# Last output tile in units of 512, 384 and 128 columns, epsilon as the logarithm's bias, a shorter Newton step, and a last pass of 640 and 384

## The chip, the core and the metric

One core of one Trainium2 chip runs the whole program in one launch. The metric is the device time of an execution in microseconds (us). The kernel before took 283.74 us (median of three runs, 282.71 to 284.28).

## What is computed

One step of a hybrid decoder trunk of depth 1. A prompt of 512 tokens and eight running sequences of one token each go through an input projection, a gated linear attention and a dilated sliding-window attention, and both mixers' outputs (`mix`, 1024 columns, 512 from each) go through one output projection and a layer norm. The change touches that last part alone:

```
mix = jnp.concatenate([o_a * silu(ga), o_b * silu(gb)], axis=-1)
y = jnp.einsum('bte,ed->btd', mix.astype(x.dtype), w_out)
x_new = layer_norm(DEEPNORM_ALPHA * x + y, ln_g, ln_b)

def layer_norm(x, g, b):
    mu = jnp.mean(xf, axis=-1, keepdims=True)
    var = jnp.mean(jnp.square(xf - mu), axis=-1, keepdims=True)
    return ((xf - mu) * lax.rsqrt(var + LN_EPS) * g + b)
```

All values are 32-bit floats, LN_EPS is 1e-5, and the norm's row of g and b is 1024 long.

## The kernel before

**Order of work.** The program is written as many small generators ("tasks"), each of which yields instructions and waits for marks that others set. A planner in the file (`Plan.run`, line 305) holds a cost for each instruction and, at every step, issues the ready instruction with the earliest start that it works out; ties go by each task's priority. So each engine's order is fixed when the program is built, by the planner's costs, and every instruction is recorded at one line (366). All matmuls of the large projections come from one task, `dense` (line 691), in a written order; the other engines' work falls between as the planner finds it ready.

**Matmuls.** Weights and activations are split into a high and a low part, and each product is three matmuls (`three`, line 618): high by high, high by low, low by high. With eight blocks of 128 in the contraction, a result tile is 24 matmuls into one PSUM bank.

**The output projection.** The 512 prompt tokens are four tiles of 128, t = 0 to 3. Tiles 0 and 1 are computed transposed (`out_first`, names ps_yf, feat_y, ps_yt). Tiles 2 and 3 come last of all matmuls, by `out_unit(t, c, w)` (line 1494): 128 tokens by w columns from column c, the activations (mha, mla, mhb, mlb) as the stationary operand and the weights (hi_wo, lo_wo) as the moving one, 24 matmuls of w columns each. Line 749 gives the units: tile 2 in two of 512, tile 3 in 512, 256 and 256.

**After a unit.** `out_evac` (line 1546), on VectorE: y = ALPHA * y + PSUM in one instruction for the unit, then one bn_stats for each 256 columns (GW) into `stats`, four of six numbers each for a row. The fourth adds `norm(t)` (line 1593): bn_aggr gives mean and variance (`mv`), and `rsqrt` (line 395) makes 1/sqrt(var + eps) in `rstd`. In the branch that the norm uses (`between` is given) VectorE adds eps to the variance, and ScalarE does Ln, Exp(-0.5 x), then a Newton step of four: Square, times x, times -0.5 plus 1.5, times the estimate. `between` is `centre`, which on VectorE does (y - mean) * gamma meanwhile. Last, VectorE does y * rstd + beta and the store is issued on SP's queue. For t = 3 the centring and the last pass are in two halves of 512 columns, each half with its own store; for the other tiles each is one instruction of 1024.

`rsqrt` without `between` (all on VectorE after Exp) serves the head norms and the eight sample rows (line 1587); that branch computes the same before and after.

Of the kernel before, what the change touches and what calls it, by code (L numbers as in the profile page):

```python
# [16 lines left out]
AF = mybir.ActivationFunctionType  # L17
ALU = mybir.AluOpType
AX = mybir.AxisListType

P = 128
# [119 lines left out]
def size(x):  # L141

    return math.prod(c for _, c in x.ap[1:])
# [51 lines left out]
class Plan:  # L195
# [14 lines left out]
    def add(self, gen, prio):  # L210
        self.seq += 1
        self.tasks.append(Task(gen, prio, self.seq))
# [158 lines left out]
def trunk(ctx: ExitStack, tc: tile.TileContext, xT, xp, xs, state, ck, cv, w_in, wab, gnorm,  # L371
# [17 lines left out]
    def bank(tag, name):  # L389
        return Need(tag, name, [P, 512])  # L390

    def cst(name, shape, dt=F32):
        return const.tile(shape, dt, name=name)

    def rsqrt(o, x, scale, eps, between=None):

        t = yield Need("m", "newton", [P, size(x)])
        t = t[:x.ap[0][1]]
        yield V.tensor_scalar(x, x, scale, eps, op0=ALU.mult, op1=ALU.add)
        yield S.activation(o, x, AF.Ln)  # L400
        yield S.activation(o, o, AF.Exp, scale=-0.5)
        if between:

            add(between, 5)
            yield S.activation(t, o, AF.Square)
            yield S.mul(t, t, x)
            yield S.activation(t, t, AF.Copy, scale=-0.5, bias=1.5)
            yield S.mul(o, o, t)
        else:
            yield V.tensor_tensor(t, o, o, op=ALU.mult)  # L410
            yield V.tensor_tensor(t, t, x, op=ALU.mult)
            yield V.tensor_scalar(x, o, -0.5, None, op0=ALU.mult)
            yield V.scalar_tensor_tensor(o, t, -3.0, x, op0=ALU.add, op1=ALU.mult)
        free(t)
# [113 lines left out]
    zw = plan.alloc(Need("t1", "zw", [P, KT, 32]))  # L528
    wz = plan.alloc(Need("t1", "wz", [P, 256]))
    one16 = cst("one16", [P, 1])  # L530

    def clear():

# [68 lines left out]

    def fills():
        yield V.memset(rb.bitcast(F32)[64:66], 1.0)
        yield At("const")
        raw = B["rb_raw"]
        yield S.copy(rb[:64], raw)
        yield V.tensor_tensor(rb[32:64], raw[32:], rb[32:64].bitcast(F32), op=ALU.subtract)
        free(raw)
        mark("rb")  # L610

        for key, shape in (("ks0", [P, 2, NP]), ("ks1", [P, 2, NP]), ("near", [P, 2, 8, 64])):
            B[key] = yield Need("g", key, shape)
            yield G.memset(B[key], 0.0)
            mark("zero_" + key)
# [75 lines left out]
    def dense():  # L691
        for _ in range(N_WARM):
            yield T.matmul(warm_ps, warm[:, :P], warm, start=True, stop=True)
        free(warm_ps)
        free(warm)

        pk = {}
        for i in range(2):
            for u in range(2):
                pk[i, u] = yield bank("ds"[i], f"ps_ka{i}{u}")  # L700
        for k in range(KT):
            for u in range(2):
                yield At("kas", k + 1)
                yield At("xs", k + 1 + (u if k == 0 else 1))
                for i in range(2):
                    yield from three(pk[i, u][:, :TW[u]], k, halves(k, u, groups[f"ka{i}"]))
        for x in ka_hl:
            free(*x)

        pz = yield bank(("t", "s"), "ps_za")  # L710
        yield At("zw")
        yield Batch(T.matmul(pz[j * 32:j * 32 + 32, :QN[j]], zw[:, k, :], xraw[k // 2][:, k % 2, Q0[j]:Q0[j] + QN[j]],
                             start=k == 0, stop=k == KT - 1, skip_group_check=True)
                    for k in range(KT) for j in range(TT))
        free(zw, *xraw)
        add(gate_decay(pz), 10)
        yield from make("ka", Need("g", "ka", [P, 2, NP]), 3)
        yield from make("qa", Need("g", "qa", [P, 2, NP]), 2)
        for i in range(2):
            for u in range(2):  # L720
                add(into("ka", ka_s, i, 1.0)(pk[i, u], u), 2)
        for i in range(2):
            yield from feature(groups[f"qa{i}"], into("qa", qa_s, i, 0.125))
        for x in ("qh0", "ql0", "qh1", "ql1"):
            yield from make(x, Need("g", x, [P, 4, 256], F32R), 4)
        for i in range(4):
            yield from feature(groups[f"qb{i}"], parts("q", q_s, i, 0.125))
        for i in range(4):
            yield from make(f"kp{i}", Need("g", f"kp{i}", [P, 2, 512], F32R), 2)
            yield from feature(groups[f"kb{i}"], parts("k", k_s, i, 1.0))  # L730
        for u in range(2):
            yield from make(f"v{u}", Need("g", f"v{u}", [P, 2, 512]))
        for i in range(2):
            yield from token(groups[f"vb{i}"], *vb_into(i))
        yield from gates("gb", gb_s)
        for u in range(2):
            yield from make(f"va{u}", Need("g", f"va{u}", [P, 2, 512]))
        for i in range(2):
            yield from token(groups[f"va{i}"], *va_into(i))
        yield from gates("ga", ga_s)  # L740
        free(*xt)
        for t in range(TT):
            add(residual(t), 8)
        add(residual_sample(), 8)
        units = [(g, f) for g in range(4) for f in range(2)]
        yield from out_first(*units[:5])
        for x in units[5:]:
            yield from out_first(x)
        for t, c, w in ((2, 0, 512), (2, 512, 512), (3, 0, 512), (3, 512, GW), (3, 768, GW)):
            yield from out_unit(t, c, w)  # L750


# [723 lines left out]
    def ln_rows():  # L1476
        yield At("y0_done", 1)
        for n, src in (("gamma", ln_g), ("beta", ln_b)):
            B[n] = yield Need("g", n, [P, DM])
            yield D.dma_start(B[n], src.to_broadcast([P, DM]))  # L1480
            mark("ln")

    def residual(t):
        if t in (2, 3):
            yield At("y0_done", 4)
        else:
            yield At("wo0_", 1)
        y = yield Need("g", f"y{t}", [P, DM])
        B["y", t] = y
        B["stats", t] = cst(f"stats{t}", [P, 4, 6])  # L1490
        yield D.dma_start(y, xp[t * P:t * P + P, :])
        mark(f"y{t}")

    def out_unit(t, c, w):
        u, tl, cs = t // 2, slice((t % 2) * P, (t % 2) * P + P), slice(c % 512, c % 512 + w)
        g = wo[c // 512]
        ps = yield bank("d", f"ps_y{t}{c // GW}")
        for k in range(KT):
            yield g.at(k)
            yield At(f"mix_b{u}{k}") if k < 4 else At(f"mix_a{u}", t % 2 + 1)  # L1500
            mh, ml = (B[f"m{x}{'ba'[k // 4]}{u}"][:, k % 4, tl] for x in "hl")
            hi, lo = g.hi[k][:, cs], g.lo[k][:, cs]
            yield from three(ps[:, :w], k, ((mh, hi), (mh, lo), (ml, hi)))
        add(out_evac(t, c // GW, ps[:, :w]), 2)

    def out_first(*units):

# [19 lines left out]
    def out_turn(g, f, ps):  # L1527
        feat = yield Need("t1", "feat_y", [P, GW])
        yield copy(feat, ps[:, :GW])
        yield copy(yts[:, 2 * g + f, :], ps[:, GW:TW[0]])  # L1530
        mark("yts")
        free(ps)
        if f == 0:
            yield from make(f"yt{g}", bank("t", f"ps_yt{g}"))
        else:
            yield At(f"yt{g}")
        for t in range(2):
            yield T.transpose(B[f"yt{g}"][:, t * GW + f * P:t * GW + f * P + P], feat[:, t * P:t * P + P], ident)
        free(feat)
        mark(f"yt_in{g}")  # L1540
        if plan.marks[f"yt_in{g}"] == 2:
            plan.share(B[f"yt{g}"], 2)
            for t in range(2):
                add(out_evac(t, g, B[f"yt{g}"][:, t * GW:t * GW + GW]), 2)

    def out_evac(t, g, ps):
        yield At(f"y{t}")
        y, st = B["y", t], B["stats", t]
        c = slice(g * GW, g * GW + size(ps))
        yield V.scalar_tensor_tensor(y[:, c], y[:, c], ALPHA, ps, op0=ALU.mult, op1=ALU.add)  # L1550
        free(ps)
        for i in range(g, g + size(ps) // GW):
            yield V.bn_stats(st[:, i, :], y[:, i * GW:i * GW + GW])
            mark(f"y{t}_done")
        if plan.marks[f"y{t}_done"] == 4:
            add(norm(t), 7 if t == 3 else 9)

    def residual_sample():
# [34 lines left out]
    def norm(t):  # L1593
        y, st = B["y", t], B["stats", t]
        mv, rstd = cst(f"mv{t}", [P, 2]), cst(f"rstd{t}", [P, 1])
        yield V.bn_aggr(mv, st.rearrange("p a b -> p (a b)"))
        ws = (512, 512) if t == 3 else (DM,)
        cs = [slice(sum(ws[:i]), sum(ws[:i]) + w) for i, w in enumerate(ws)]

        def centre():  # L1600
# [7 lines left out]
        for i, c in enumerate(cs):  # L1608
            yield At(f"centred{t}", i + 1)
            yield V.scalar_tensor_tensor(y[:, c], y[:, c], rstd, B["beta"][:, c], op0=ALU.mult, op1=ALU.add)  # L1610
            yield D.dma_start(y_p[t * P:t * P + P, c], y[:, c])
        free(y)


# [142 lines left out]
```

## Time and profile before

| | |
|---|---|
| median of three runs | 283.74 us (282.71 to 284.28) |
| the profiled execution, its own time | 282.88 us |
| its span, first to last instruction | 281.0 us |
| TensorE busy, share of the span | 270.9 us, 96% |
| TensorE's granted clock, mean | 0.992 |
| first matmul of tile 3, last one of all | 261.99 us, 273.11 us |
| last pass of tile 3 on VectorE begins | 276.42 us |
| issue of the last two stores on SP | 277.20 us and 277.87 us |

The profiled execution is 0.86 us under the median. What lies around its span is 282.88 - 281.0 = 1.9 us. In the rows quoted below, a timeline row is: start (us from the span's start), length (us), engine, line, operation, out<-in, partitions x elements of out and in, count, and in brackets how long the engine had been idle and who ended that. PE is TensorE's matmuls, PEld its weight loads, DVE is VectorE, ACT ScalarE, SPq the queue on which SP issues DMAs, ACTq the one on which ScalarE does. Rows of one engine with the same operation and names are merged into one. A row of a group has operation, out<-in, and either minimum/median/maximum in ns with the first and last start, or busy us and the mean ns of one. Buffer numbers are left out of the names: `y` is the residual tile of whichever t.

### The profile page before, as it was taken

What the parts mean: (1) busy time and instruction counts of PE and PEld (TensorE: products, weight loads), DVE (VectorE), ACT (ScalarE), POOL (GpSimd) and SP (SyncE); (2) the same over time, 40 slices, a digit from 0 to 9 for tenths busy, and PEclk for the clock granted to TensorE, in tenths of its full rate; (3) what the DMA queues carried; (4) which work ended last, traced back from release to release, by engine and by line L of the source; (5) the groups of instructions that cost most, each with busy time, mean ns of one, the idle gap of its engine ahead of it and who ended that gap; (6) DMA issues with size and microseconds to landing.
All of it is one profiled execution on the core that took longest, in us unless ns stands there. A gap on an engine that the chain in (4) does not pass through costs nothing.

```text
span 281.0 us, 7058 instructions
## 1 busy us (share of the span) xinstructions
PE 270.9 (96%) x2760; PEld 253.0 (90%) x2760; DVE 206.4 (73%) x496; ACT 157.6 (56%) x453; POOL 53.1 (19%) x72
## 2 busy tenths in 40 slices
PE   8899999999999999999999999999999999999990
PEld 5799999999999998988879999999899999997880
DVE  4747798998969975728949966617989889239575
ACT  5747853544475856738949735425589986113011
POOL 4000000000296065400006244444400000000000
PEclk9999999999999999999999999999999999999996
DMA  6996622382894897723977398997674993976203
GB/s 190 298 241 179 200 77 77 78 225 79 236 330 148 250 306 216 223 81 88 303 210 198 111 264 207 249 224 175 221 199 125 250 264 107 240 108 200 113 27 124
DMA packets 59944, 52.27 MB, mean 186 GB/s; under 512 B 12506, under 2 KB 50692, under 8 KB 59910
## 3 DMA queue, kind: packets, MB, share of 16 engines
q1 hardware_dynamic: 59802, 51.73, 66.2%
q8 instruction: 22, 0.36, 0.6%
q14 instruction: 12, 0.10, 0.1%
q10 hardware_dynamic: 108, 0.07, 0.1%
HBM read 46.24 MB, written 6.03 MB: 186 GB/s over the span
## 4 chain that ended last, share of the span: by engine, by line
PE 90%; DVE 5%; DMA 3%; ACT 1%; issue 0%; SPq 0%; DVEq 0%
PE ps_gb L366 8%; PE ps_qb L366 8%; PE ps_yf L366 8%; PE ps_y L366 8%; PE ps_ga L366 7%; PE ps_kb L366 7%; PE ps_vb_f L366 4%; PE ps_qa L366 4%; PE ps_va_f L366 4%; PE ps_va L366 4%; PE ps_vb L366 4%; PE ps_pt L366 3%; PE ps_pv L366 3%; PE ps_s L366 3%; PE ps_ka L366 3%; DMA x_raw<-in_xT_dram 3%
## 5 line engine op out<-in xcount | busy, mean ns | idle before, releaser
L366 POOL TENSOR_TENSOR past<-past,qbc 128x256 f32<-128x256 f32 x32 | 24.9, 814 | 87.5 <-DMA past<-in_ck_dram 86.3
L366 POOL TENSOR_TENSOR vv<-vv,pb 128x256 f32<-128x256 f32 x32 | 25.0, 812 | 58.5 <-DVE mlb L366 32.2
L366 ACT ACTIVATE pr<-pr,ms 128x128 f32<-128x128 f32 (+3 forms) x47 | 24.4, 538 | 9.0 <-DVE ms L366 8.8
L366 DVE CUSTOM_DVE_ANT_0 pr<-ps_s,strip 128x128 f32<-128x128 f32 (+3 forms) x32 | 14.2, 481 | 6.7 <-PE ps_s L366 6.5
L366 PE MATMUL ps_ka<-xx,hi_ka 128*128 128x264 f32 (+1 forms) x64 | 13.6, 309 | 1.1 <-ACT xx L366 0.8
L366 ACT ACTIVATE sg<-sg 128x264 f32<-128x264 f32 (+1 forms) x32 | 13.6, 425 | 0.3
L366 PE MATMUL ps_pt<-cf,pr 128*128 128x128 f32 x80 | 13.4, 277 | 0.0
L366 PEld LDWEIGHTS ps_ka<-xx,hi_ka 128*128 128x128 f32 x64 | 11.0, 206 | 2.1 <-ACT xx L366 1.0
L366 ACT COPY pt<-ps_pt 128x128 f32<-128x128 f32 (+3 forms) x26 | 10.7, 422 | 1.1 <-PE ps_pt L366 1.0
L366 PEld LDWEIGHTS ps_pt<-cf,pr 128*128 128x128 f32 x80 | 9.2, 140 | 1.7 <-issue 1.2
L366 ACT ACTIVATE rstd<-mv 128x1 f32<-128x1 f32 x4 | 0.7, 203 | 16.6 <-DVE mv L366 16.6
L366 DVE TENSOR_REDUCE o_pv<-vv 128x4 f32<-128x1024 f32 x8 | 9.7, 1212 | 0.0
L366 DVE TENSOR_REDUCE lt<-past 128x16 f32<-128x1024 f32 x8 | 9.6, 1202 | 0.0
L366 PE MATMUL ps_pv<-pt,v 128*64 128x256 f32 (+1 forms) x96 | 9.5, 348 | 0.0
L366 PE MATMUL ps_ka<-xx,lo_ka 128*128 128x264 f32 (+1 forms) x32 | 9.4, 295 | 0.0
L366 ACT COPY feat_y<-ps_yf 128x256 f32<-128x256 f32 x8 | 2.9, 368 | 11.1 <-PE ps_yf L366 11.1
L366 PEld LDWEIGHTS ps_pv<-pt,v 128*64 128x64 f32 x96 | 6.3, 137 | 2.9
L366 DVE TENSOR_TENSOR xx<-x_raw,xx 128x520 fp32r<-128x520 f32 (+2 forms) x9 | 5.8, 640 | 3.6 <-ACT xx L366 3.5
L366 PE MATMUL ps_s<-kp,qh 64*128 64x128 f32 (+3 forms) x64 | 8.3, 344 | 0.0
L366 ACT ACTIVATE d<-d 128x512 f32<-128x512 f32 x11 | 6.6, 640 | 2.9 <-DVE d L366 2.9
L366 DVE TENSOR_SCALAR pr<-pr,ms 128x512 f32<-128x512 f32 (+2 forms) x17 | 8.1, 486 | 0.2
L366 DVE COPY_PREDICATED near<-cm,ps_l 128x256 f32<-128x256 uint8 x12 | 6.2, 544 | 1.9 <-PE ps_l L366 1.8
(530 smaller groups left out, 1031.3 us busy)
## 6 DMA issues: line engine op xcount, KB each, us to landing
past<-in_ck_dram SPq DMA_DIRECT2D x8, 512.0 KB
vv<-in_cv_dram SPq DMA_DIRECT2D x8, 512.0 KB
pb<-psd_s SPq DMA_DIRECT2D x16, 256.0 KB
s<-in_state_dram SPq DMA_DIRECT2D x4, 512.0 KB
qbc<-qsd SPq DMA_DIRECT2D x8, 256.0 KB
strip<-tabr SPq DMA_DIRECT2D x8, 256.0 KB
y<-in_xp_dram SPq DMA_DIRECT2D x4, 512.0 KB
x_raw<-in_xT_dram SPq DMA_DIRECT2D x7, 260.0 KB
```

The source lines that it names most:

```text
L366: getattr(eng.eng, op.fn)(*op.args, **op.kw)
```

## The change

Five edits, all at the end of the program or in the norm that ends it:

1. Tile 3 is computed in units of 512, 384 and 128 columns instead of 512, 256 and 256.
2. For tile 3 bn_stats goes by 128 columns (`part_of`), eight instructions instead of four, and bn_aggr then reads 48 numbers a row instead of 24.
3. In `rsqrt` with `between` (all four tiles), Ln takes the raw variance with eps as its bias (a new constant column `ln_eps`, written once at the program's start). The instruction on VectorE now makes -0.5 * (var + eps), named newton in the rows, beside ScalarE's Ln and not ahead of it. The Newton step is three operations: Square, then one Copy with that column as scale and 1.5 as bias, then times the estimate.
4. Tile 3's centring and last pass are 640 and 384 columns instead of 512 and 512.
5. Tile 3's first store (640 columns) is issued on ScalarE's queue, the second on SP's as before.

```diff
--- before.py
+++ after.py
@@ -394,19 +394,21 @@
 
     def rsqrt(o, x, scale, eps, between=None):
 
-        t = yield Need("m", "newton", [P, size(x)])
-        t = t[:x.ap[0][1]]
-        yield V.tensor_scalar(x, x, scale, eps, op0=ALU.mult, op1=ALU.add)
-        yield S.activation(o, x, AF.Ln)
-        yield S.activation(o, o, AF.Exp, scale=-0.5)
+        n = size(x)
+        t = yield Need("m", "newton", [P, 2 * n])
+        t, half = t[:x.ap[0][1], :n], t[:x.ap[0][1], n:]
         if between:
-
+            yield S.activation(o, x, AF.Ln, scale=scale, bias=ln_eps)
+            yield V.tensor_scalar(half, x, -0.5 * scale, -0.5 * eps, op0=ALU.mult, op1=ALU.add)
+            yield S.activation(o, o, AF.Exp, scale=-0.5)
             add(between, 5)
             yield S.activation(t, o, AF.Square)
-            yield S.mul(t, t, x)
-            yield S.activation(t, t, AF.Copy, scale=-0.5, bias=1.5)
+            yield S.activation(t, t, AF.Copy, scale=half, bias=1.5)
             yield S.mul(o, o, t)
         else:
+            yield V.tensor_scalar(x, x, scale, eps, op0=ALU.mult, op1=ALU.add)
+            yield S.activation(o, x, AF.Ln)
+            yield S.activation(o, o, AF.Exp, scale=-0.5)
             yield V.tensor_tensor(t, o, o, op=ALU.mult)
             yield V.tensor_tensor(t, t, x, op=ALU.mult)
             yield V.tensor_scalar(x, o, -0.5, None, op0=ALU.mult)
@@ -528,6 +530,7 @@
     zw = plan.alloc(Need("t1", "zw", [P, KT, 32]))
     wz = plan.alloc(Need("t1", "wz", [P, 256]))
     one16 = cst("one16", [P, 1])
+    ln_eps = cst("ln_eps", [P, 1])
 
     def clear():
 
@@ -602,6 +605,7 @@
 
     def fills():
         yield V.memset(rb.bitcast(F32)[64:66], 1.0)
+        yield V.memset(ln_eps, LN_EPS)
         yield At("const")
         raw = B["rb_raw"]
         yield S.copy(rb[:64], raw)
@@ -746,7 +750,7 @@
         yield from out_first(*units[:5])
         for x in units[5:]:
             yield from out_first(x)
-        for t, c, w in ((2, 0, 512), (2, 512, 512), (3, 0, 512), (3, 512, GW), (3, 768, GW)):
+        for t, c, w in ((2, 0, 512), (2, 512, 512), (3, 0, 512), (3, 512, 384), (3, 896, P)):
             yield from out_unit(t, c, w)
 
 
@@ -1480,6 +1484,9 @@
             yield D.dma_start(B[n], src.to_broadcast([P, DM]))
             mark("ln")
 
+    def part_of(t):
+        return P if t == 3 else GW
+
     def residual(t):
         if t in (2, 3):
             yield At("y0_done", 4)
@@ -1487,21 +1494,21 @@
             yield At("wo0_", 1)
         y = yield Need("g", f"y{t}", [P, DM])
         B["y", t] = y
-        B["stats", t] = cst(f"stats{t}", [P, 4, 6])
+        B["stats", t] = cst(f"stats{t}", [P, DM // part_of(t), 6])
         yield D.dma_start(y, xp[t * P:t * P + P, :])
         mark(f"y{t}")
 
     def out_unit(t, c, w):
         u, tl, cs = t // 2, slice((t % 2) * P, (t % 2) * P + P), slice(c % 512, c % 512 + w)
         g = wo[c // 512]
-        ps = yield bank("d", f"ps_y{t}{c // GW}")
+        ps = yield bank("d", f"ps_y{t}{c // P}")
         for k in range(KT):
             yield g.at(k)
             yield At(f"mix_b{u}{k}") if k < 4 else At(f"mix_a{u}", t % 2 + 1)
             mh, ml = (B[f"m{x}{'ba'[k // 4]}{u}"][:, k % 4, tl] for x in "hl")
             hi, lo = g.hi[k][:, cs], g.lo[k][:, cs]
             yield from three(ps[:, :w], k, ((mh, hi), (mh, lo), (ml, hi)))
-        add(out_evac(t, c // GW, ps[:, :w]), 2)
+        add(out_evac(t, c, ps[:, :w]), 2)
 
     def out_first(*units):
 
@@ -1541,18 +1548,18 @@
         if plan.marks[f"yt_in{g}"] == 2:
             plan.share(B[f"yt{g}"], 2)
             for t in range(2):
-                add(out_evac(t, g, B[f"yt{g}"][:, t * GW:t * GW + GW]), 2)
-
-    def out_evac(t, g, ps):
+                add(out_evac(t, g * GW, B[f"yt{g}"][:, t * GW:t * GW + GW]), 2)
+
+    def out_evac(t, c, ps):
         yield At(f"y{t}")
-        y, st = B["y", t], B["stats", t]
-        c = slice(g * GW, g * GW + size(ps))
-        yield V.scalar_tensor_tensor(y[:, c], y[:, c], ALPHA, ps, op0=ALU.mult, op1=ALU.add)
+        y, st, w = B["y", t], B["stats", t], part_of(t)
+        cs = slice(c, c + size(ps))
+        yield V.scalar_tensor_tensor(y[:, cs], y[:, cs], ALPHA, ps, op0=ALU.mult, op1=ALU.add)
         free(ps)
-        for i in range(g, g + size(ps) // GW):
-            yield V.bn_stats(st[:, i, :], y[:, i * GW:i * GW + GW])
+        for i in range(c // w, cs.stop // w):
+            yield V.bn_stats(st[:, i, :], y[:, i * w:i * w + w])
             mark(f"y{t}_done")
-        if plan.marks[f"y{t}_done"] == 4:
+        if plan.marks[f"y{t}_done"] == DM // w:
             add(norm(t), 7 if t == 3 else 9)
 
     def residual_sample():
@@ -1594,7 +1601,7 @@
         y, st = B["y", t], B["stats", t]
         mv, rstd = cst(f"mv{t}", [P, 2]), cst(f"rstd{t}", [P, 1])
         yield V.bn_aggr(mv, st.rearrange("p a b -> p (a b)"))
-        ws = (512, 512) if t == 3 else (DM,)
+        ws = (640, 384) if t == 3 else (DM,)
         cs = [slice(sum(ws[:i]), sum(ws[:i]) + w) for i, w in enumerate(ws)]
 
         def centre():
@@ -1608,7 +1615,7 @@
         for i, c in enumerate(cs):
             yield At(f"centred{t}", i + 1)
             yield V.scalar_tensor_tensor(y[:, c], y[:, c], rstd, B["beta"][:, c], op0=ALU.mult, op1=ALU.add)
-            yield D.dma_start(y_p[t * P:t * P + P, c], y[:, c])
+            yield (S if t == 3 and i == 0 else D).dma_start(y_p[t * P:t * P + P, c], y[:, c])
         free(y)
```

What the planner makes of it on VectorE, from tile 3's first unit on (y_3909 is tile 2, y_3911 tile 3; ps_y is the unit's bank). Before:

```order
L366 SCALAR_TENSOR_TENSOR y_3911<-y_3911,ps_y_3996 128x512
L366 BN_AGGR mv_4039<-stats_3910 128x2
L366 BN_STATS stats_3912<-y_3911 128x6 x2
L366 TENSOR_SCALAR mv_4039<-mv_4039 128x1
L366 SCALAR_TENSOR_TENSOR y_3909<-y_3909,mv_4039,gamma 128x1024
L366 SCALAR_TENSOR_TENSOR y_3911<-y_3911,ps_y_4025 128x256
L366 BN_STATS stats_3912<-y_3911 128x6
L366 SCALAR_TENSOR_TENSOR y_3909<-y_3909,rstd_4040,beta 128x1024
L366 SCALAR_TENSOR_TENSOR y_3911<-y_3911,ps_y_4062 128x256
```

And with the change, the same stretch of VectorE (y_3911 is now tile 2, y_3913 tile 3):

```order
L366 SCALAR_TENSOR_TENSOR y_3913<-y_3913,ps_y_3996 128x512
L366 BN_AGGR mv_4037<-stats_3912 128x2
L366 BN_STATS stats_3914<-y_3913 128x6 x4
L366 TENSOR_SCALAR newton<-mv_4037 128x1
L366 SCALAR_TENSOR_TENSOR y_3911<-y_3911,mv_4037,gamma 128x1024
L366 SCALAR_TENSOR_TENSOR y_3911<-y_3911,rstd_4038,beta 128x1024
L366 SCALAR_TENSOR_TENSOR y_3913<-y_3913,ps_y_4025 128x384
L366 BN_STATS stats_3914<-y_3913 128x6 x3
L366 SCALAR_TENSOR_TENSOR y_3913<-y_3913,ps_y_4070 128x128
L366 BN_STATS stats_3914<-y_3913 128x6
```

Tile 2's last pass now stands ahead of the evacuation of tile 3's second unit, where it stood between the second unit and the third.

On ScalarE, the last rows of the program (tile 3's norm). Before:

```order
L366 ACTIVATE rstd_4101<-mv_4100 128x1
L366 ACTIVATE rstd_4101<-rstd_4101 128x1
L366 ACTIVATE newton<-rstd_4101 128x1
L366 ACTIVATE newton<-newton,mv_4100 128x1
L366 ACTIVATE newton<-newton 128x1
L366 ACTIVATE rstd_4101<-rstd_4101,newton 128x1
```

And with the change, the same place:

```order
L366 ACTIVATE rstd_4104<-mv_4103,ln_eps 128x1
L366 ACTIVATE rstd_4104<-rstd_4104 128x1
L366 ACTIVATE newton<-rstd_4104 128x1
L366 ACTIVATE newton<-newton 128x1
L366 ACTIVATE rstd_4104<-rstd_4104,newton 128x1
L366 DMA out_dram<-y_3913 128x640
```

Six activations have become five, the first of them reads one operand more, and behind them stands the store of 640 columns, which SP's queue has lost. TensorE's order is the same up to tile 3's second unit; there 48 matmuls of 256 columns become 24 of 384 and 24 of 128. POOL's order does not change, and nothing ahead of tile 0's norm does but the one memset.

## The prediction, on record before the changed kernel ran

> **What bounds the kernel now.** I read the page's busy times first, then the chain that ended last.
>
> ```profile
> PE 270.9 (96%) x2760; PEld 253.0 (90%) x2760; DVE 206.4 (73%) x496; ACT 157.6 (56%) x453; POOL 53.1 (19%) x72
> PE 90%; DVE 5%; DMA 3%; ACT 1%; issue 0%; SPq 0%; DVEq 0%
> ```
>
> TensorE is busy for 270.9 of 281.0 us and 90% of the chain is its matmuls. All that the change touches lies where that chain leaves TensorE: the last matmuls and what follows them. So I read TensorE's timeline next, at the start of tile 3, of its first 256-column unit, and at the last matmul.
>
> ```profile
> 261.99 0.39 PE L366 MATMUL ps_y<-hi_wo__3152,mhb 128*128 128x512 f32 x1
> ...
> 267.56 0.28 PE L366 MATMUL ps_y<-hi_wo__3412,mhb 128*128 128x256 f32 x1
> ...
> 273.11 0.28 PE L366 MATMUL ps_y<-hi_wo__3646,mla 128*128 128x256 f32 x1
> ```
>
> A unit is 24 matmuls. The 512-column unit takes 267.56 - 261.99 = 5.57 us, 0.232 a matmul; the 48 matmuls of the two 256-column units have 47 intervals in 273.11 - 267.56 = 5.55 us, 0.118 each. Each length (0.28, 0.39) is a latency; the intervals are the cost. Now what stands behind the last matmul, first on VectorE:
>
> ```profile
> 267.76 0.69 DVE L366 SCALAR_TENSOR_TENSOR y<-y,ps_y 128x512 f32<-128x512 f32 x1 [3.35 <-PE ps_y L366]
> 268.37 0.26 DVE L366 BATCH_NORM_AGGREGATE mv<-stats 128x2 f32<-128x24 f32 x1
> 268.54 0.70 DVE L366 BATCH_NORM_STATS2 stats<-y 128x6 f32<-128x256 f32 x2
> 269.16 0.14 DVE L366 TENSOR_SCALAR mv<-mv 128x1 f32<-128x1 f32 x1
> 269.21 1.28 DVE L366 SCALAR_TENSOR_TENSOR y<-y,mv,gamma 128x1024 f32<-128x1024 f32 x1
> ...
> 271.40 1.27 DVE L366 SCALAR_TENSOR_TENSOR y<-y,rstd,beta 128x1024 f32<-128x1024 f32 x1
> 273.43 0.42 DVE L366 SCALAR_TENSOR_TENSOR y<-y,ps_y 128x256 f32<-128x256 f32 x1 [0.76 <-PE ps_y L366]
> 273.88 0.43 DVE L366 BATCH_NORM_STATS2 stats<-y 128x6 f32<-128x256 f32 x1
> 274.35 0.26 DVE L366 BATCH_NORM_AGGREGATE mv<-stats 128x2 f32<-128x24 f32 x1
> 274.64 0.15 DVE L366 TENSOR_SCALAR mv<-mv 128x1 f32<-128x1 f32 x1
> 274.71 1.40 DVE L366 SCALAR_TENSOR_TENSOR y<-y,mv,gamma 128x512 f32<-128x512 f32 x2
> 276.42 1.41 DVE L366 SCALAR_TENSOR_TENSOR y<-y,rstd,beta 128x512 f32<-128x512 f32 x2 [0.31 <-ACT rstd L366]
> ```
>
> VectorE has been idle 0.76 us when the last unit arrives, so TensorE sets 273.43. From there the work is serial, and before its last pass VectorE waits 0.31 us for ScalarE's `rstd`. ScalarE's rows, the first being the end of tile 2's norm, and the issue of the stores:
>
> ```profile
> 270.60 0.29 ACT L366 ACTIVATE rstd<-rstd,newton 128x1 f32<-128x1 f32 x1
> 274.83 0.20 ACT L366 ACTIVATE rstd<-mv 128x1 f32<-128x1 f32 x1 [3.94 <-DVE mv L366]
> ...
> 275.54 0.29 ACT L366 ACTIVATE newton<-newton,mv 128x1 f32<-128x1 f32 x1
> 275.86 0.20 ACT L366 ACTIVATE newton<-newton 128x1 f32<-128x1 f32 x1
> 276.10 0.29 ACT L366 ACTIVATE rstd<-rstd,newton 128x1 f32<-128x1 f32 x1
> ```
>
> ```profile
> 277.20 0.99 SPq L366 DMA_DIRECT2D out_dram<-y  x2
> ```
>
> Six activations in a row take 276.42 - 274.83 = 1.59 us. The two issues of the stores, merged into the last row, begin at 277.20. The last view is the DMA's, from there to 280, in 40 slices of 0.07 us, busy tenths:
>
> ```profile
> DMA  0000000000006999998999799999789620000000
> ```
>
> Data moves from slice 12 (278.03) to slice 32 (279.5), some 1.5 us, near 9 tenths busy: the two stores make one stretch, 0.83 us behind the first issue, and the engines are never free between them.
>
> **The change, part by part, in order of time.**
>
> *Units of 384 and 128.* Columns in all are the same, so it rests on a 128-column matmul's interval. No matmul over the whole array with 128 moving columns of these split operands is in the trace; the nearest are the scores (ps_s), on half the rows, two side by side.
>
> ```profile
> 72.73 0.27 PE L366 MATMUL ps_s<-kp,ql 64*128 64x128 f32 x2
> 72.84 0.45 PE L366 MATMUL ps_s<-kp,qh 64*128 64x256 f32 x4
> ...
> 110.59 0.34 PE L366 MATMUL ps_s<-kp,ql 64*128 64x384 f32 x2
> 110.77 0.62 PE L366 MATMUL ps_s<-kp,qh 64*128 64x512 f32 x3
> ```
>
> A pair with 128 columns takes 72.84 - 72.73 = 0.11 us, so each half of the array needs 0.11 a matmul; a pair with 384 takes 0.18, which agrees with the middle of 0.118 and 0.232, 0.175. So 384 is paid by its columns and 128 is not: it costs about what 256 costs. The weight loads, by their stationary columns (32, 64, 128, and 128 in a transpose; the number behind min/median/max or the comma is ns):
>
> ```profile
> L366 PEld LDWEIGHTS ps_za<-x_raw,zw x64: 106/110/110, 19.1 to 20.8; 128*32 128x32 f32 x64
> L366 PEld LDWEIGHTS ps_pv<-pt,v 128*64 128x64 f32 x96 | 6.3, 137 | 2.9
> L366 PEld LDWEIGHTS ps_kb<-xx,hi_kb__838 128*128 128x128 f32 x32 | 4.9, 189 | 0.0
> L366 PEld LDWEIGHTS ps_pt<-cf,pr 128*128 128x128 f32 x80 | 9.2, 140 | 1.7 <-issue 1.2 <-ACT mhb L366 0.4
> ```
>
> 110 ns for 32 columns, 137 for 64 and 189 for 128 is 0.8 ns a column, so I read 128 stationary columns as streaming for about 0.105 us whatever the matmul does. Under 256 moving columns that is hidden; under 128 it is not. The transposes' load of 128 columns, 140 ns, speaks against it, but these are plain 32-bit values in a transpose, not the split parts. I take 0.110 and 0.175: 24 x 0.175 + 24 x 0.110 = 6.84 us, against 48 x 0.118 = 5.67. **TensorE ends 1.17 us later.** Bounds: 0.061 for a matmul paid by its columns alone (256 columns more cost 0.114, so 128 fewer than 256 cost 0.118 - 0.057), which ends TensorE where it ended; and 0.118, the price of 256 columns, +1.4.
>
> The Trainium skill, "TensorE: Matmul & The Clock Gate", section "Back-to-back issue gap", gives about 81 ns a matmul for load-and-matmul pairs at N = 128, which lies between the bounds. No row here shows it; it is a rival below.
>
> *The first and second unit's tail.* bn_stats of 128 columns, four after the first unit and three after the second, cost VectorE more instructions (two of 256 take 0.70, 0.35 each; at 0.13 less, as worked out below, four take 0.9). Cover: the second unit now reaches VectorE at 267.56 + 4.20 + 0.3 = 272.1. Tile 2's last pass, now ahead of it, can start when the centring (269.4 to 270.7) is done and rstd is there (270.9 before, earlier now), and ends at 272.0; the 384-column evacuation and three bn_stats end by 273.5. The last unit comes at 274.6: 1.1 us to spare. Without that cover each would add its own length. Tile 2's store on SP is issued some 0.7 us earlier, at about 272.0, well ahead of the last ones. Nothing on TensorE waits for this.
>
> *The last evacuation and bn_stats.* 512 columns take 0.69 and 256 take 0.42: 0.27 for 256, so 128 columns save 0.13. bn_stats exists only at 256 (0.43); by the same price a column it saves 0.13 (between 0 and half of 0.43). bn_aggr reads 48 numbers instead of 24 in 0.26: +0.03 by that price, at most +0.26. **-0.23.**
>
> *Epsilon and Newton.* TENSOR_SCALAR leaves the chain: Ln starts at its place, 274.64 and not 274.83, -0.19. Ln has a second operand: with one column as operand an activation takes 0.29 and not 0.20, +0.09. The multiply by x goes (275.86 - 275.54 = -0.32), and the Copy's scale becomes a column, +0.09. ScalarE's part: -0.33. But what is late next? VectorE still does the TENSOR_SCALAR and both centrings, 274.64 to 276.11, 1.50 us after bn_aggr's end at 274.61; ScalarE would now be ready 1.48 after it. So the last pass starts some 1.52 after bn_aggr, not 1.81. **-0.29** (0 to -0.33). For tiles 0 to 2 the same saving is worth nothing: TensorE runs past them. The memset of `ln_eps` falls into VectorE's idle time at the start (its first memsets end before 2 us, and x is converted from 3.2 us on).
>
> *Last pass 640 and 384, first store on ScalarE's queue.* The first store's issue comes 128 columns later, +0.13; both stores move the same data in one stretch of about 1.5 us behind it, so the end shifts by the start: **+0.13**. The smaller second store gains nothing, since its data waits for the first's anyway. ScalarE has nothing left to do, so the queue is free. Bounds: 0 if the two queues pack better, and, from ScalarE's only DMAs so far, at the program's start:
>
> ```profile
> L366 ACTq DMA_DIRECT2D wz<-in_wab_dram x4: 279/320/583, 1.4 to 2.9; - x4
> DMA packets 231, 0.22 MB, mean 161 GB/s; under 512 B 16, under 2 KB 231, under 8 KB 231
> q1 hardware_dynamic: 231, 0.22, 56.8%
> ```
>
> These four were issued from 1.4 on; from there to 2.79 us (the window of the two last rows) all 231 packets are of SP's queue, q1. So ScalarE's first DMA waited 1.35 us at least, where the last stores wait 0.83: up to +0.5 more.
>
> The Trainium skill, "Trainium Kernel Development and Optimization", section "Key Constraints", has it that queues of SP and ScalarE share the same 16 DMA engines and that issuing from several saves the issue time alone. By that rule the split is worth nothing here, as in the sum, since SP's issue never held the second store; with two independent paths the 384 columns would end by themselves, 1.45 (last pass) + 0.83 + 3/8 of 1.5 = 2.85 us behind the last pass's start, where the data ended 3.1 us behind it, and this term would be -0.25. The trace's one unbroken stretch speaks for the rule.
>
> *Sum:* 1.17 - 0.23 - 0.29 + 0.13 = **+0.78 us**. The profiled execution would go from 282.88 to 283.7, its span to 281.8. That execution was 0.86 under the median of the three runs, so against the median the forecast is 283.74 + 0.8 = **284.5 us**, 0.3% slower. A measurement of this kernel tells about 0.5%, 1.4 us, from no change; the forecast lies within that.
>
> **Rivals.**
>
> *The 128-column matmul is paid by its columns* (0.061). The place is the last unit. For it: the units of 256 and 512 fit a price per column, and the transposes load 128 columns in 140 ns. Against it: the pair of ps_s. TensorE ends where it did, the sum is -0.39: 283.35, faster. The point from which the sign turns: the tail saves 0.39 net, so 24 x (0.175 + s) = 5.67 + 0.39, s = 0.078 us.
>
> *0.081 a matmul.* TensorE's end +0.47, the sum +0.08: 283.8. That is no change at all. Against it again stands 0.11.
>
> *ScalarE's queue is late.* One mechanism, slower: the store of 640 columns starts up to 0.5 us later, and its issue takes 0.58 as the first did, not 0.33, another 0.25. The sum becomes +1.3 to +1.5: 285.0 to 285.2. It decides as soon as ScalarE's first packet comes more than about 0.5 us later than SP's did. For it: that queue has been idle since 5 us, as it was at the start. Against it: at the start several things were cold at once.
>
> *The shorter chain is longer.* bn_aggr at twice the numbers (+0.26), the centring bound by VectorE: the gain of the norm goes, +1.2: 284.9. Within the forecast's range.
>
> **How the numbers follow.** Forecast (weight loads bind, 283.9 to 285.1): 0.60. Column price: 0.10. 0.081: 0.08. ScalarE's queue late: 0.15. Something that this trace doesn't show: 0.07. The range leaves out the tenth below and the tenth above: 283.1 to 285.5; below lie the column price's best and half of the unseen, above the worst of the late queue and the rest. Slower by over 0.5% (above 285.16): half of the late queue (0.07), the upper edge of the forecast with the runs' own spread of 0.8 us either side (0.13), and most of the unseen: 0.25. Faster by over 0.5%: the lower edges, 0.05. Within: 0.70.
>
> **What would show it.** In the changed profile: 24 matmuls of 384 columns 0.175 apart, then 24 of 128 columns 0.11 apart, the last one at 274.3; if these are 0.061 apart the main step is wrong. VectorE idle for about a microsecond before the last evacuation; Ln right behind bn_aggr; five activations in 1.45 us; the last pass 1.5 us after bn_aggr; the stores' data in one stretch, beginning 0.83 us after ScalarE's issue and ending 1.5 us later. A first packet of ScalarE's queue over 1.3 us behind its issue, or VectorE still at bn_stats when the last unit arrives, would make the prediction too low.

## The result, and the profile after

| | before | changed |
|---|---|---|
| median, 13 runs each | 283.74 us | 284.45 us |
| lowest to highest | 282.71 to 284.28 | 284.04 to 285.10 |
| ratio, 95% interval | 1 | 1.0032 [1.0019, 1.0046] |
| the profiled execution: its own time, its span | 282.88, 281.0 us | 284.59, 282.7 us |
| tile 3's first matmul | 261.99 us | 262.87 us |
| its second unit's first matmul to the span's end ("the tail") | 13.40 us | 14.26 us |

The change costs 0.3%: 0.71 us between the medians, 0.9 by the ratio. The forecast was 0.8 us and 284.5. The profiled execution also reaches tile 3 0.9 us later than before's did, with the same instructions in the same order up to tile 0's norm (from 253.7 us on before) but for one memset. The experiments come back to that; the tail, which holds all that the five edits do to tile 3, is 0.86 us longer. TensorE's timeline of the changed kernel, at the first matmul of each unit of tile 3 and the last one of all (start, length, names, shape):

```profile
262.87 0.39 PE L366 MATMUL ps_y<-hi_wo__3154,mhb 128*128 128x512 f32 x1
...
268.45 0.33 PE L366 MATMUL ps_y<-hi_wo__3414,mhb 128*128 128x384 f32 x1
...
272.66 0.22 PE L366 MATMUL ps_y<-hi_wo__3414,mhb 128*128 128x128 f32 x1
...
275.17 0.28 PE L366 MATMUL ps_y<-hi_wo__3648,mla 128*128 128x128 f32 x1
```

The 384-column unit takes 272.66 - 268.45 = 4.21 us, 0.175 a matmul. The 128-column unit has 23 intervals in 275.17 - 272.66 = 2.51 us, 0.109 each: half the columns of a 256-column matmul, and hardly less than its 0.118. From the second unit's first matmul to the last one it is 6.72 us, where it was 5.55. VectorE from tile 3's first evacuation on:

```profile
268.65 0.69 DVE L366 SCALAR_TENSOR_TENSOR y<-y,ps_y 128x512 f32<-128x512 f32 x1 [3.35 <-PE ps_y L366]
269.25 0.26 DVE L366 BATCH_NORM_AGGREGATE mv<-stats 128x2 f32<-128x24 f32 x1
269.43 0.82 DVE L366 BATCH_NORM_STATS2 stats<-y 128x6 f32<-128x128 f32 x4
...
271.60 1.28 DVE L366 SCALAR_TENSOR_TENSOR y<-y,rstd,beta 128x1024 f32<-128x1024 f32 x1
272.85 0.55 DVE L366 SCALAR_TENSOR_TENSOR y<-y,ps_y 128x384 f32<-128x384 f32 x1
273.44 0.68 DVE L366 BATCH_NORM_STATS2 stats<-y 128x6 f32<-128x128 f32 x3
275.48 0.29 DVE L366 SCALAR_TENSOR_TENSOR y<-y,ps_y 128x128 f32<-128x128 f32 x1 [1.36 <-PE ps_y L366]
275.81 0.29 DVE L366 BATCH_NORM_STATS2 stats<-y 128x6 f32<-128x128 f32 x1
276.13 0.37 DVE L366 BATCH_NORM_AGGREGATE mv<-stats 128x2 f32<-128x48 f32 x1
276.54 0.15 DVE L366 TENSOR_SCALAR newton<-mv 128x1 f32<-128x1 f32 x1
276.61 1.40 DVE L366 SCALAR_TENSOR_TENSOR y<-y,mv,gamma 128x640 f32<-128x640 f32 x2
277.99 1.41 DVE L366 SCALAR_TENSOR_TENSOR y<-y,rstd,beta 128x640 f32<-128x640 f32 x2
```

VectorE now sits idle for 1.36 us before the last unit comes (0.76 before): it has finished all that lies ahead, and TensorE sets the start. From the last evacuation to bn_aggr it is 0.65 us and not 0.92. The last pass no longer has a bracket: VectorE's second centring runs, by its recorded length, until the pass begins, and ScalarE's last activation ends 0.03 us before that. ScalarE's end of the program:

```profile
276.54 0.29 ACT L366 ACTIVATE rstd<-mv,ln_eps 128x1 f32<-128x1 f32 x1 [5.53 <-DVE mv L366]
276.87 0.20 ACT L366 ACTIVATE rstd<-rstd 128x1 f32<-128x1 f32 x1
277.10 0.20 ACT L366 ACTIVATE newton<-rstd 128x1 f32<-128x1 f32 x1
277.33 0.29 ACT L366 ACTIVATE newton<-newton 128x1 f32<-128x1 f32 x1
277.66 0.29 ACT L366 ACTIVATE rstd<-rstd,newton 128x1 f32<-128x1 f32 x1
278.91 0.38 ACTq L366 DMA_DIRECT2D out_dram<-y  x1
```

Ln starts together with VectorE's TENSOR_SCALAR (276.54) and not behind it, and five activations take 277.99 - 276.54 = 1.45 us. The DMAs from that issue (278.9) on, 40 slices of 0.07 us, and the two queues (ScalarE's is q10):

```profile
DMA  0000000000004699799899798899999961000000
...
q10 hardware_dynamic: 144, 0.33, 30.1%
q1 hardware_dynamic: 144, 0.20, 18.6%
```

Data from slice 12 to slice 33, 1.5 us without a hole: two queues, and still one stretch that begins where the first store lets it.

### The profile page after: what moved, and what is told of

Its sections match the earlier page's. It is cut to its first block, busy times and chain, and to the rows that moved or that the text cites. A ratio compares the mean times of both kernels' runs of the same rounds, so it can differ in the third digit from the quotient of the medians.

```text
span 282.7 us, 7064 instructions
## 1 busy us (share of the span) xinstructions
PE 271.7 (96%) x2760; PEld 253.5 (90%) x2760; DVE 204.6 (72%) x501; ACT 157.6 (56%) x449; POOL 54.4 (19%) x72
## 4 chain that ended last, share of the span: by engine, by line
PE 88%; DMA 5%; DVE 3%; SPq 1%; ACT 1%; issue 1%; DVEq 0%
PE ps_y L366 8%; PE ps_qb L366 8%; PE ps_gb L366 8%; PE ps_ga L366 8%; PE ps_yf L366 8%; PE ps_kb L366 6%; PE ps_vb_f L366 4%; PE ps_qa L366 4%; PE ps_va_f L366 4%; PE ps_va L366 4%; PE ps_vb L366 4%; PE ps_pt L366 3%; PE ps_pv L366 3%; PE ps_s L366 3%; DMA x_raw<-in_xT_dram 2%; PE ps_l L366 2%
## 5 line engine op out<-in xcount | busy, mean ns | idle before, releaser
L366 POOL TENSOR_TENSOR vv<-vv,pb 128x256 f32<-128x256 f32 x32 | 26.8, 868 | 56.6 <-DVE ms L366 33.1
L366 PE MATMUL ps_ka<-xx,hi_ka 128*128 128x264 f32 (+1 forms) x64 | 12.8, 297 | 1.2 <-DVE xx L366 0.7
L366 PEld LDWEIGHTS ps_ka<-xx,hi_ka 128*128 128x128 f32 x64 | 10.3, 193 | 2.2 <-DVE xx L366 1.1
L366 ACT ACTIVATE rstd<-mv,ln_eps 128x1 f32<-128x1 f32 x4 | 1.1, 290 | 17.4 <-DVE mv L366 17.4
```

The source lines that it names most:

```text
L366: getattr(eng.eng, op.fn)(*op.args, **op.kw)
```

## The experiments

Every ratio is to the kernel before, run on the same chip. Theory W is the forecast's, that 24 matmuls of 128 columns are bound by their weight loads; the rivals are named in the expectations. The tail is the row of the table above, from each run's own profile.

### The units undone: e1_units_back

```diff
-(3, 0, 512), (3, 512, 384), (3, 896, P)
+(3, 0, 512), (3, 512, GW), (3, 768, GW)
```

> The changed kernel with one edit undone: tile 3 in units of 512, 256 and 256 again (bn_stats still by 128, Newton, epsilon and the last pass as changed). Theory W (the 24 matmuls of 128 columns are bound by their weight loads): TensorE ends 1.2 us earlier than in the changed kernel, the last evacuation and bn_stats take 0.35 us more, so about 0.8 us faster than the changed kernel: ratio to before 1.000 (0.999 to 1.001). Rival U (the loss lies ahead of tile 3, where the changed kernel's profile is 0.89 us later than before's, through the new constants and buffers): ratio stays near 1.003. Rival S (the loss is the last pass and ScalarE's store): ratio stays near 1.003, with the stores' data ending 3.3 us or more behind the last pass's start.

Ratio 1.0006 [0.9986, 1.0026], tail 13.42 us. VectorE at the last unit:

```profile
274.53 0.42 DVE L366 SCALAR_TENSOR_TENSOR y<-y,ps_y 128x256 f32<-128x256 f32 x1 [0.81 <-PE ps_y L366]
274.99 0.48 DVE L366 BATCH_NORM_STATS2 stats<-y 128x6 f32<-128x128 f32 x2
275.50 0.37 DVE L366 BATCH_NORM_AGGREGATE mv<-stats 128x2 f32<-128x48 f32 x1
```

The bracket is back at 0.81, the last evacuation and bn_stats take 0.97 and not 0.65, and the tail is within 0.02 us of before's: the loss is gone. All new constants and the new stores are still there, so neither rival carries the loss of the tail; the whole time alone, with an interval up to 1.0026, would not have shown it.

### The units alone: e2_units_only, and again: e9_units_again

The diff's hunks on `out_unit`, `out_evac`, `part_of` and the list of units, on the kernel before; `rsqrt` and the last pass as before.

> The kernel before with only the units of 512, 384 and 128 (and bn_stats by 128 for tile 3); the norm and the last pass as before. Theory W: TensorE's last matmul starts 6.7 us after the second unit's first, not 5.55; evacuation and bn_stats 0.65 and not 0.92, bn_aggr 0.37 and not 0.26: +1.0 us, ratio 1.0035 (1.002 to 1.005). Rivals U and S: no constant but the larger stats is new and the last pass is that of before, so ratio 1.000, with the same 1.2 us on TensorE hidden or absent.

> The units of 512, 384 and 128 alone, once more, beside the changed kernel on one chip: the whole times of the parts added to less than the changed kernel's loss, where the rows of the tail added up. Theory W: the runs' spread ahead of tile 3 did it, and this comes out at 1.002 to 1.005, 0.1 to 0.2% above the changed kernel. Rival I (the parts do something together that they don't do alone): 1.0016 again, and the changed kernel at 1.003 or more, above it.

Tails 14.37 and 14.36 us, +0.96, as W had it. The whole times say less: 1.0016 [0.9999, 1.0033] and 1.0021 [1.0002, 1.0040], where 0.96 us would be 1.0034. The first lies below the 1.002 to 1.005 that W gave.

### Epsilon and Newton alone: e3_newton_only, and again: e12_newton_again

The hunk on `rsqrt` and the constant `ln_eps`, on the kernel before.

> The kernel before with only epsilon as Ln's bias and the Newton step of three operations. Theory W: from bn_aggr's end to the last pass 1.5 us and not 1.81, everything behind it as before: -0.3 us, ratio 0.999 (0.998 to 1.000). Rival U: the new constant moves buffers, ratio above 1.001 with tile 3 beginning later. Rival S: as W here.

> Epsilon as the logarithm's bias and the Newton step of three operations alone, once more, as the version that came out under both kernels. Theory W: from the second unit to the end 13.06 us, 0.34 less than before, ratio 0.999; if the 0.9981 of the first time was in part the runs' spread, this comes out nearer to 0.999. Rival S: as W. Rival U: no statement.

Ratios 0.9981 [0.9967, 0.9995] and 0.9976 [0.9954, 0.9998]; tails 13.06 both times, 0.34 less. VectorE of the first of the two:

```profile
274.40 0.26 DVE L366 BATCH_NORM_AGGREGATE mv<-stats 128x2 f32<-128x24 f32 x1
274.69 0.15 DVE L366 TENSOR_SCALAR newton<-mv 128x1 f32<-128x1 f32 x1
274.77 1.41 DVE L366 SCALAR_TENSOR_TENSOR y<-y,mv,gamma 128x512 f32<-128x512 f32 x2
276.15 1.41 DVE L366 SCALAR_TENSOR_TENSOR y<-y,rstd,beta 128x512 f32<-128x512 f32 x2
```

From bn_aggr's start to the last pass 276.15 - 274.40 = 1.75 us, where it was 2.08. This version beats the kernel before, by 0.2%: the medians are 282.88 us beside 283.59 in the first run, 282.82 beside 283.72 in the second. By the ratios it is 0.5% under the changed kernel. The tail gives 0.34 us, 0.1%; the second ratio came out further from W's 0.999, not nearer, and both intervals hold that value.

### The last pass alone: e4_last_pass_only

```diff
-        ws = (512, 512) if t == 3 else (DM,)
+        ws = (640, 384) if t == 3 else (DM,)
-            yield D.dma_start(y_p[t * P:t * P + P, c], y[:, c])
+            yield (S if t == 3 and i == 0 else D).dma_start(y_p[t * P:t * P + P, c], y[:, c])
```

> The kernel before with only the last pass and the centring in 640 and 384 columns and the first store on ScalarE's queue. Theory W: +0.15 to +0.2 us (the first store is issued 0.13 us later and the data ends 3.3 us, not 3.13, behind the last pass's start), ratio 1.0006 (0.9995 to 1.0015). Rival S: the whole loss is here, ratio 1.003 or more. Rival U: ratio 1.000.

Ratio 1.0005 [0.9989, 1.0020], tail 13.58 us, +0.17. The data ends 3.31 us behind the last pass's start, 3.13 before. A small loss, a fifth of the changed kernel's by the tail.

### Its two halves: e6_640_both_sp and e7_512_first_act

The first has only the `ws` line of the diff above, the second only the line with the store. One execution each, so their rows are read and not their whole times.

> The kernel before with the last pass in 640 and 384 columns and both stores on SP's queue. Theory W (the start of the first store sets the end): the data ends 3.25 us behind the last pass's start, as far as with ScalarE's queue or 0.05 less. If two queues were what makes the stores overlap, the second store's data would begin later here and the end be 0.2 us later.

> The kernel before with the last pass in two of 512 columns and only the first store moved to ScalarE's queue. If ScalarE's queue is as quick as SP's, the first packet comes 0.83 us behind the issue and the data ends 3.13 us behind the last pass's start, as before. If that queue is late (0.88 in the changed kernel's profile), 0.05 us later.

Data ends 3.26 us behind the last pass's start with 640 and 384 columns on SP's queue, and 3.19 us with 512 and 512 and the first store on ScalarE's; 3.13 before. The DMAs of e6_640_both_sp, 40 slices of 0.07 us from its first issue:

```profile
DMA  0000000000017997999997999999999620000000
```

One stretch again, now on one queue, begun 0.13 us later behind the last pass's start as the longer first part demands. Of the +0.18 with both, 0.13 is the 640 columns and 0.05 is ScalarE's queue: its first packet came 0.88 us behind its issue, SP's 0.83.

### The disputed matmul by itself: e5_probe

```diff
+        mh, mh6 = B["mhb1"][:, 0, :P], B["mhb1"][:, 0, :64]
+        ps = yield bank("d", "ps_probe")
+        for m, n in ((mh, 512), (mh, 384), (mh, 256), (mh, 192), (mh, 128), (mh, 64), (mh6, 256), (mh6, 128), (mh6, 64)):
+            for _ in range(24):
+                yield T.matmul(ps[:size(m), :n], m, wo[1].hi[0][:, :n], start=True, stop=True)
```

> The kernel before, with 216 matmuls added behind the last unit into a spare bank that nothing reads: 24 each of the same stationary tile of 128 columns with 512, 384, 256, 192, 128 and 64 moving columns, then 24 each of 64 stationary columns with 256, 128 and 64. Theory W (a load streams its stationary columns at 0.8 ns each): with 128 stationary columns the intervals are 0.232, 0.175, 0.118, then a floor of 0.11 for 192, 128 and 64; with 64 stationary columns 0.118 for 256, and 0.06 to 0.07 for 128 and 64. Rival F (a fixed cost of each matmul, whatever its weights): 0.11 with 64 stationary columns too. Rival C (columns alone): 0.09, 0.06 and 0.03 to 0.04 for 192, 128 and 64 with 128 stationary columns.

TensorE inside the stages (one row from each of seven windows: the first start, the length to the last one's end, the count):

```profile
281.21 3.11 PE L366 MATMUL ps_probe<-hi_wo__3412,mhb 128*128 128x384 f32 x17
285.03 2.41 PE L366 MATMUL ps_probe<-hi_wo__3412,mhb 128*128 128x256 f32 x19
287.83 2.28 PE L366 MATMUL ps_probe<-hi_wo__3412,mhb 128*128 128x192 f32 x19
290.48 2.29 PE L366 MATMUL ps_probe<-hi_wo__3412,mhb 128*128 128x128 f32 x19
293.02 1.84 PE L366 MATMUL ps_probe<-hi_wo__3412,mhb 128*128 128x64 f32 x15
302.09 0.88 PE L366 MATMUL ps_probe<-hi_wo__3412,mhb 128*64 128x128 f32 x12
303.01 1.39 PE L366 MATMUL ps_probe<-hi_wo__3412,mhb 128*64 128x64 f32 x21
```

Less the last one's latency (0.34, 0.28, 0.27 and so on, 0.22 for 64 stationary columns) and over one interval fewer than the count: 0.173 for 384, 0.118 for 256, then 0.112, 0.112 and 0.112 for 192, 128 and 64 moving columns. With 64 stationary columns it is 0.060 for 128 moving columns and 0.058 for 64. The floor is there, it begins between 256 and 192 moving columns, and it halves with the stationary columns: so it is neither the moving columns (rival C) nor a fixed cost of a matmul (rival F), but the load. The disputed 128 moving columns cost 0.060 as soon as the load is half as long, which is the prediction's price by columns alone (0.061); the rest of their 0.112 is the load's. Two weight-load groups of the same probe, 64 and 128 columns:

```profile
L366 PEld LDWEIGHTS ps_probe<-hi_wo__3412,mhb 128*64 128x64 f32 x21 | 1.3, 138 | 0.0
L366 PEld LDWEIGHTS ps_probe<-hi_wo__3412,mhb 128*128 128x128 f32 x18 | 2.1, 192 | 0.0
```

138 and 192 ns: 54 ns for 64 columns more, the same 0.84 ns a column. The Trainium skill, "TensorE: Matmul & The Clock Gate", section "LDWEIGHTS (loading the stationary operand)", puts a load's time in ns at its columns over 1.2, whatever its rows. That makes an estimate of 107 ns for 128 columns and 53 for 64; the probe agrees with 0.112 and 0.058 us. The 81 ns at N = 128 that the Trainium skill gives on the same page, "TensorE: Matmul & The Clock Gate", section "Back-to-back issue gap", was not seen here: it was 109 to 112 ns.

The stage with 64 stationary and 256 moving columns is left out: the granted clock was halved in it. The next one, with 128 moving columns, began so too (0.52 from 301.0 to 301.7 us); its row above starts at 302.09, where the clock is back at 1.00 (the last section has the windows).

### The suspected cost twice: e8_two_128

```diff
-(3, 0, 512), (3, 512, 384), (3, 896, P)
+(3, 0, 512), (3, 512, GW), (3, 768, P), (3, 896, P)
```

on the units alone.

> The kernel before with tile 3 in units of 512, 256, 128 and 128 (bn_stats by 128), norm and last pass as before: the suspected cost twice. Theory W (the price is the load of 128 stationary columns, 0.11 us a matmul, paid by each matmul however few columns follow): TensorE's last matmul 24 x (0.118 + 0.11 + 0.11) = 8.1 us behind the second unit's first, so +2.6 us there, and from the second unit to the end 13.40 + 2.6 - 0.27 + 0.11 = 15.8 us; ratio 1.0085 (1.007 to 1.010). Column price: 5.7 us there, ratio 0.999. Rival U (what lies ahead of tile 3): ratio as of the units alone, 1.0016.

Ratio 1.0067 [1.0042, 1.0093], tail 15.67 us, +2.27. The last two units of TensorE, first and last matmul of each:

```profile
270.29 0.22 PE L366 MATMUL ps_y<-hi_wo__3412,mhb 128*128 128x128 f32 x1
...
272.80 0.27 PE L366 MATMUL ps_y<-hi_wo__3646,mla 128*128 128x128 f32 x1
272.91 0.28 PE L366 MATMUL ps_y<-hi_wo__3412,mhb 128*128 128x128 f32 x1
...
275.48 0.27 PE L366 MATMUL ps_y<-hi_wo__3646,mla 128*128 128x128 f32 x1
```

Intervals of 0.109 and 0.112. Columns are the same, matmuls 24 more, and it costs as many loads: from the second unit's first matmul to the last one 8.04 us, where W had 8.1. The ratio is just under the 1.007 to 1.010 that W gave; 2.27 us more would be 1.0080, within the interval.

### What lies ahead of tile 3: e10_changed_again and e11_constants_only

e10 is the changed kernel once more. e11 is the kernel before with `ln_eps`, its memset, and tile 3's statistics as a tile of 8 x 6 of which half is used; nothing reads `ln_eps`.

> The changed kernel once more, beside the two others. Theory W: ratio 1.0025 to 1.0035, below the units alone by 0.1 to 0.2%. Rival I: above the units alone.

> The kernel before with the changed kernel's two constants and nothing else: the column of epsilon with its memset (which nothing reads) and tile 3's statistics in a tile of 8 x 6, of which the first half is used. So every later buffer stands where it does in the changed kernel, and the instructions are those of before. Rival U in its last form (the buffers' new places cost the stretch ahead of tile 3 some time, which would be why the changed kernel came out 0.2% above the units alone although its tail is shorter): ratio 1.0015 to 1.0025, tile 3 beginning later than in before's profile by 0.5 us or more. Theory W: 1.000 (0.9985 to 1.0015), the tail from the second unit to the end 13.40 us.

The changed kernel came out at 1.0045 [1.0030, 1.0061], tail 14.25; the units alone beside it at 1.0021. So by whole times it stands above the units alone, as rival I had it and against W's 1.0025 to 1.0035, though its tail is 0.11 us shorter. The tails of the parts (+0.96, -0.34, +0.17) add to 0.79, 0.07 under the changed kernel's 0.86. Most of that is that with the units alone the stores' data ended 3.09 us behind the last pass's start, where it was 3.13 before; why is not shown. The constants are not the reason: e11 is at 0.9992 [0.9976, 1.0008], tail 13.39. What is left varies from one execution to the next, and it arises early. The first matmul of the scores (the first start in these rows) comes 1.0 us later in the changed kernel's profile than in before's, a little more than tile 3's does:

```profile
L366 PE MATMUL ps_s<-kp,qh x64: 271/332/442, 72.5 to 147.2; 64*128 64x128 f32 x16, 64*128 64x256 f32 x16, 64*128 64x384 f32 x16, 64*128 64x512 f32 x16
L366 PE MATMUL ps_s<-kp,qh x64: 271/332/442, 73.5 to 148.3; 64*128 64x128 f32 x16, 64*128 64x256 f32 x16, 64*128 64x384 f32 x16, 64*128 64x512 f32 x16
```

It comes at 73.9 and 74.0 in e6 and e7, which have none of the new constants, and from there to tile 3 all profiles agree within 0.6 us. The same program, Newton alone, began tile 3 at 262.04 in one profile and at 264.46 in the other:

```profile
262.04 0.39 PE L366 MATMUL ps_y<-hi_wo__3154,mhb 128*128 128x512 f32 x1
```

```profile
264.46 0.39 PE L366 MATMUL ps_y<-hi_wo__3154,mhb 128*128 128x512 f32 x1
```

In the later one the granted clock fell for some microseconds near the start. The windows 8 to 12 and 12 to 16 us, with PE's busy time and count, the granted clock, the DMA share and GB/s, of the first profile and then of the second:

```profile
8.00:12.00 4.00, 3.65 (x30) 1.00 0.99 320
12.00:16.00 4.00, 4.00 (x36) 1.00 0.87 196
```

```profile
8.00:12.00 4.00, 2.42 (x18) 1.00 1.00 341
12.00:16.00 4.00, 4.00 (x23) 0.57 0.72 160
```

No other profile has such a fall there. TensorE had been busy for 2.42 of the 4 us before it, for 2.90 or more in all others; that this was the reason is not shown. Over the other profiles tile 3 began at 261.4 to 263.7 us, and the tails of the same program agree within 0.02. Whether a steady 0.1 to 0.2% lies ahead of tile 3 in some of these programs stays open: the intervals of the whole times are as wide as the difference.

## Why the prediction was right

| step of the sum | forecast | measured |
|---|---|---|
| TensorE's end, 384 and 128 | +1.17 us | +1.17 (6.72 against 5.55) |
| last evacuation and bn_stats | -0.26 | -0.27 |
| bn_aggr on 48 numbers | +0.03 | +0.11 |
| epsilon and Newton | -0.29 | -0.33 (e3: 1.75 against 2.08) |
| last pass and stores | +0.13 | +0.18 (e4: +0.17) |
| sum | +0.78 | +0.86, the tail |

**The weight loads.** Right in kind and size, and shown three ways: undone, doubled, and by itself with half the stationary columns. The step that mattered was to take the price of a matmul not seen before from the scores on half the array, 0.11 a pair, and not from the columns. Before's trace had a nearer row that the forecast passed over. It took the transposes' short load, 140 ns, as speaking against it; but they too have 128 moving columns over the whole array, and four in a row stand

```profile
152.67 0.60 PE L366 MATMUL ps_pt<-cf,pr 128*128 128x128 f32 x4
```

(0.60 - 0.27) / 3 = 0.11 us apart, 0.27 being the last one's latency. Their values are not the split ones, so they are near and not the same; but their spacing is that of the changed kernel's 128 columns, and the recorded length of a load told nothing of it.

**The tail's savings.** Right. VectorE had more than the 1.1 us to spare that was forecast, 1.36. **bn_aggr** was mis-sized: 24 numbers more cost 0.11 us, 4.5 ns each, not the 1 ns of a column. That lies within the bound given (+0.26).

**What is late next.** I had VectorE's centring set the last pass. ScalarE still does: its last activation ends at 277.96 and the pass starts at 277.99; 0.02 to 0.03 us lie between any two instructions of this chain. The second centring's recorded length runs to 278.01, but on VectorE the next instruction starts before such a length ends: the two centrings, 0.87 and 0.61 us long, fill 1.40, so the second began 0.08 early. By that overlap VectorE could have begun the pass at about 277.93. So the gain was the whole -0.33.

**The stores.** Right that two queues make one stretch and that its begin sets the end. The rival of the late queue fell: 0.05 us and not 0.5; what ScalarE's DMAs did at the program's start was no measure for its end.

**The other rivals.** Paid by columns, and 0.081, both fell to the probe.

**The whole time.** That the change stays within 0.5% held: the interval ends at 1.0046. The second run of the changed kernel, up to 1.0061, does not exclude a little more. That the median came within 0.1 us of the forecast's 284.5 is in part luck: in that second run the medians are 1.41 us apart (284.66 and 283.25), where the tail is 0.85 us longer.

## What to carry to other kernels

A narrow last unit shortens the work behind it by its columns, but each of its matmuls pays its weight load: here 192, 128 and 64 moving columns all cost 0.112 us a matmul with 128 stationary ones, and 256 cost 0.118. By the step from 384 to 256 (0.0045 us for each ten columns) the floor begins at about 240, an estimate. So the remainder is to be cut no narrower than what hides the load. Take the price of a shape that the trace lacks from the row nearest in what binds it, not from the size. And of edits that come in one change, each wants its own term: here one of them, alone, came out faster than the kernel before, and the whole slower.

## What the runs showed that was not expected

bn_aggr's price of 4.5 ns a number (0.263 us for 24, 0.371 for 48). And in the probe the granted clock fell to half behind the main work, with TensorE busy throughout: windows of the probe, with PE's busy time and count, the granted clock, the DMA share and GB/s:

```profile
288.00:295.00 7.00, 7.00 (x65) 0.99 0.01 2
294.00:295.00 1.00, 1.00 (x11) 0.92 0.00 0
296.00:301.00 5.00, 5.00 (x25) 0.50 0.00 0
302.00:304.00 2.00, 2.00 (x38) 1.00 0.00 0
```

The fall comes within the second window, in the last matmuls with 64 moving columns; the third holds the 24 matmuls of 256 moving columns, 0.21 us each instead of 0.118. Why the clock fell just there was not tried.
